# A fused decoder layer on one core: the recurrent block's input tiles ahead of its gate tiles, its products on VectorE, and a recut last norm

## The chip, the cores and the metric

The kernel runs on 1 core of a Trainium2 chip. The metric is device time in microseconds of one execution: the median of three runs for the kernel before. One more execution was recorded by the hardware profiler; all views quoted here are of that one.

## The reference

One decoder layer over 512 positions of width 1024 in float32: a norm, one wide projection, three token mixers (a chunked gMLP, a sparse attention, a gated linear recurrence), a gated sum of the three through branch weights, an output projection with a norm, and a SwiGLU block with a norm. The change touches the recurrence and the last norm above all:

```
def rglru_mixer(xr, gate, conv_w, conv_b, w_a, b_a, w_x, b_x, lam):
    xc = causal_conv4(xr, conv_w) + conv_b
    xh = xc, by heads
    r = sigmoid(einsum('bshi,hio->bsho', xh, w_a) + b_a)
    i = sigmoid(einsum('bshi,hio->bsho', xh, w_x) + b_x)
    log_a = -LRU_C * r * softplus(-lam)
    a = exp(log_a)
    b_in = sqrt(-expm1(2.0 * log_a)) * (i * xc)
    h = scan of h[t] = a[t] * h[t-1] + b_in[t]
    return h * gelu(gate)

...
f = (silu(f_gate) * f_up) @ w_ffn_out
return x + f * rsqrt(mean(f * f) + EPS) * g_post_ffn
```

(Shortened; casts are left out.)

## The kernel before

**Tiles.** Every matrix product keeps float32 accuracy by splitting both factors into a high and a low part (hi and lo, xh and xl) and adding three products: hi with xh, hi with xl, lo with xh. A tile of the projection is 128 output channels by 512 positions; with 8 blocks of the inner dimension that is 24 matmuls of 128x512 into one bank `mm` of PSUM (`passes`, L212; `matrix`, L216). The input of the projection is hh and hl, the normed x.

**Weights.** They stream tile by tile in the order of `wlist` (L124 to L161). `wload` (L166) issues the DMA of a 512 KB tile into one of two raw buffers from SyncE (SP), ScalarE (ACT) copies out hi (L114) and VectorE (DVE) subtracts lo (L119). `unit` (L201) asks for two tiles ahead.

**Order.** A list of main generators (each one a tile) and one side generator are woven by `run` (L1157): after every group of 6 matmuls the side generator may advance, at the given rate, and a tile that yields a number w is set aside and resumed w steps later, between the matmuls of the next tiles. The calls of `run` stand at L1202 to L1209. Tile's scheduler then fixes the order of instructions for each engine; each engine works through its own list in order and waits on semaphores.

**The recurrence** has 8 channel tiles in two halves of four. For each there is an input tile, `xr_tile` (L410): 24 matmuls, then a causal convolution (ACT L420, three DVE passes L422), a split into ch and cl, six matmuls L430 with the block-diagonal gate weights wabh and wabl into two `tr` banks, a sigmoid into R (L432), a tanh into TI (L435) and a DVE product with xc (L436). And there is a gate tile of the recurrence, `rg_tile` (L460): 24 matmuls and a gelu in four passes (`gelu2`, L383 to L390) into GG. Per half, `rec_batch` (L439) makes T and the decay a on ACT (tanh, sqrt, exp), a DVE product (L454), a GpSimd (POOL) product (L455) and the scan on DVE (L457); `rec_out` (L466) multiplies with GG on POOL (L473) and splits the result into ych and ycl, the input of the branch product. Input and gate tiles alternate within a half, with `gate_tile` (the three branch gates of the attention heads, L586) and two `cmp_tile` (L606, inputs of the compressed keys and values) between the halves, beside which the first half's recurrence runs.

**Around it.** `norm` (L326) finishes hh and hl under the first tiles `v_half`; `softplus` (L359) is a polynomial of some 26 small DVE operations; `compress` (L627) loads the compression weights w1 with two DMAs from ACT (L630), adds the position codes on POOL (L638) and multiplies on PE (L648 to L676); `gmlp_prep` (L480) loads two tables gw for the gMLP (L483, L484), masks one on POOL (L485) and scales the other on DVE (L487).

**The end.** `down` (L1103) accumulates the last product for four blocks of 128 rows, in two halves f of 512 columns each. `close` (L1125) squares and sums a block's rows on ACT (L1128), and in the second half forms the reciprocal root, multiplies by the gain gf and by the root, adds the residual and stores the rows.

## Time and profile before

| what | us |
|---|---|
| median of three runs | 1164.91 |
| the three runs | 1162.02, 1165.14, 1164.91 |
| the profiled execution | 1168.17 |
| its span, first to last instruction | 1166.4 |
| busy: PE, DVE, ACT, POOL | 1140.9, 690.6, 532.8, 55.2 |
| mean granted PE clock | 0.991 of full speed |

The profile's page draws the span in 40 equal slices of 29.2 us; a digit is the busy share in tenths, and PEclk the granted clock in tenths:

```profile
PE   9999799999999999999999999999999999999997
DVE  5974855545476799998898743557333323322324
POOL 0000702510000000000000000000000000000001
PEclk9999989899999999999999999999999999999999
```

PE is full but for one slice early on, the fifth (117 to 146 us), which is also the one in which POOL works most; the sixth and the eighth show a clock below the others. A timeline row reads: start, duration (both us), engine, line, operation, output <- inputs by name, shape, count, and in brackets how long the engine had been idle and what it had waited for. A row that ends in x3 sums three.

### The profile page before, as it was taken

Reading aid. Unit: us, or ns where it says so; the run is one execution under the profiler, and the core shown is the slowest. Engines: PE = TensorE matmul, PEld = TensorE weight load, DVE = VectorE, ACT = ScalarE, POOL = GpSimd, SP = SyncE. Lnnn points to the kernel's source line nnn. Section 1 sums busy time; section 2 is a strip of 40 time slices with the busy share of each in tenths; the row PEclk is TensorE's granted clock in tenths of the full one; section 3 lists DMA queues with packets and bytes.
Section 4 is the critical chain, followed back from the end, with each engine's and each line's share of the span. In section 5 each row is a group of like instructions: output and inputs, shape, how many; then the busy total and the mean of one; then the engine's idle time right before and its main releaser. Section 6 shows DMA issues by size and latency. Waiting matters only on the chain.

```text
span 1166.4 us, 14306 instructions
## 1 busy us (share of the span) xinstructions
PE 1140.9 (98%) x5524; PEld 949.6 (81%) x5524; DVE 690.6 (59%) x1266; ACT 532.8 (46%) x936; POOL 55.2 (5%) x55
## 2 busy tenths in 40 slices
PE   9999799999999999999999999999999999999997
PEld 7877578788888887888888788889988888888885
DVE  5974855545476799998898743557333323322324
ACT  6746446222244576877776523344323223232222
POOL 0000702510000000000000000000000000000001
PEclk9999989899999999999999999999999999999999
DMA  8332222522222211112111343332132232232231
GB/s 286 116 108 73 69 76 65 209 92 90 94 87 91 72 55 37 55 41 69 37 55 55 110 145 107 116 119 73 55 103 96 91 106 93 92 125 91 93 106 72
DMA packets 30373, 108.62 MB, mean 93 GB/s; under 512 B 3649, under 2 KB 3793, under 8 KB 29153
## 3 DMA queue, kind: packets, MB, share of 16 engines
q1 hardware_dynamic: 27792, 98.58, 25.7%
q10 hardware_dynamic: 2448, 9.05, 2.1%
q8 instruction: 43, 0.70, 0.2%
q14 instruction: 26, 0.20, 0.1%
q0 software_dynamic: 64, 0.08, 0.0%
HBM read 105.60 MB, written 2.10 MB: 92 GB/s over the span
## 4 chain that ended last, share of the span: by engine, by line
PE 87%; DVE 7%; DMA 3%; ACT 2%; issue 1%; POOL 1%; SPq 0%; DVEq 0%; ACTq 0%; POOLq 0%
PE mm L212 57%; PE mm L1122 10%; PE mm L1022 4%; PE sc L816 3%; PE o L854 3%; PE tr L841 3%; PE mm L732 2%; DVE lo L119 1%; PE tr L648 1%; PE tr L430 1%; DMA wabr<-in_wab 1%; DMA xrow<-in_x 1%; DVE ti L457 1%; PE tr L564 1%; DMA xt<-in_xT 1%
## 5 line engine op out<-in xcount | busy, mean ns | idle before, releaser
L114 ACT ACTIVATE hi<-raw 128x1024 fp32r<-128x1024 f32 (+1 forms) x162 | 170.8, 1054 | 357.6 <-PE mm L212 160.7
L119 DVE TENSOR_TENSOR lo<-raw,hi 128x1024 fp32r<-128x1024 f32 (+1 forms) x162 | 199.6, 1233 | 220.4 <-ACT hi L114 212.6
L212 PE MATMUL mm<-hh,lo 128*128 128x512 f32 x504 | 199.5, 396 | 2.5 <-DVE lo L119 2.5
L212 PE MATMUL mm<-hh,hi 128*128 128x512 f32 x504 | 200.5, 398 | 0.0
L212 PE MATMUL mm<-hl,hi 128*128 128x512 f32 x504 | 198.8, 395 | 0.0
L212 PE MATMUL mm<-fh,hi 128*128 128x512 f32 (+1 forms) x336 | 127.6, 380 | 0.0
L212 PE MATMUL mm<-fh,lo 128*128 128x512 f32 (+1 forms) x336 | 127.3, 379 | 0.0
L212 PE MATMUL mm<-fl,hi 128*128 128x512 f32 (+1 forms) x336 | 127.3, 379 | 0.0
L212 PEld LDWEIGHTS mm<-hh,lo 128*128 128x128 f32 x504 | 95.7, 190 | 22.8 <-DVE lo L119 3.4
L212 PEld LDWEIGHTS mm<-hl,hi 128*128 128x128 f32 x504 | 95.5, 189 | 18.9 <-issue 0.2
L212 PEld LDWEIGHTS mm<-hh,hi 128*128 128x128 f32 x504 | 95.6, 190 | 18.8 <-issue 0.2
L1122 PE MATMUL mm<-hi,f 128*128 128x512 f32 x320 | 99.4, 389 | 0.0
L822 ACT ACTIVATE P<-P,ast 128x128 f32<-128x128 f32 (+3 forms) x128 | 70.7, 555 | 23.2 <-DVE ast L820 22.6
L212 PEld LDWEIGHTS mm<-fh,lo 128*128 128x128 f32 x336 | 63.2, 188 | 12.0
L212 PEld LDWEIGHTS mm<-fh,hi 128*128 128x128 f32 x336 | 63.2, 188 | 11.8
L212 PEld LDWEIGHTS mm<-fl,hi 128*128 128x128 f32 x336 | 63.2, 188 | 11.7
L1122 PEld LDWEIGHTS mm<-hi,f 128*128 128x128 f32 x320 | 60.1, 188 | 12.4
L820 DVE CUSTOM_DVE_ANT_0 P<-sc,mask 128x128 f32<-128x128 f32 (+3 forms) x128 | 58.0, 485 | 8.2 <-PE sc L816 7.3
L1122 PE MATMUL mm<-lo,f 128*128 128x512 f32 x160 | 62.2, 389 | 0.0
L114 ACT ACTIVATE ph<-tr 128x512 fp32r<-128x512 f32 x80 | 47.0, 592 | 26.2 <-PE tr L841 25.2
L1079 DVE TENSOR_TENSOR silu<-silu,mm 128x512 f32<-128x512 f32 x22 | 15.1, 688 | 73.1 <-PE mm L212 73.1
L119 DVE TENSOR_TENSOR pl<-tr,ph 128x512 fp32r<-128x512 f32 x80 | 54.4, 686 | 2.8 <-ACT ph L114 1.0
(295 smaller groups left out, 1941.8 us busy)
## 6 DMA issues: line engine op xcount, KB each, us to landing
raw<-in_w_in SPq DMA_DIRECT2D x64, 512.0 KB, 3.5
raw<-in_w_fi SPq DMA_DIRECT2D x44, 512.0 KB, 3.5
raw<-in_w_br SPq DMA_DIRECT2D x24, 512.0 KB, 3.5
raw<-in_w_fo SPq DMA_DIRECT2D x22, 512.0 KB, 3.5
w<-in_cw ACTq DMA_DIRECT2D x4, 1024.0 KB, 6.6
raw<-in_w_o SPq DMA_DIRECT2D x8, 512.0 KB, 3.6
...
xt<-in_xT SPq DMA_DIRECT2D x8, 256.0 KB, 7.4
```

The lines of the kernel that those rows point to most:

```text
L114: SC.activation(hi, src, AF.Copy)
L119: res["lo"] = V.tensor_sub(lo, src, f32(hi))
L212: res["mm"] = PE.matmul(ps[:m, n0:n1], w[:, k * 128:k * 128 + m], x[k][:, n0:n1], start=(t == 0), stop=(t == 3 * NK - 1))
L732: PE.matmul(ps, x[k][:, q], w[:, ws], start=(k == 0 and t == 0), stop=(k == NK - 1 and t == 2))
L816: PE.matmul(ps[:, :w * n].rearrange("p (b n) -> p b n", b=w), lhs, K[:, i, brs[0]:brs[-1] + 1, :n], start=(i == 0), stop=(i == 1))
L820: V.tensor_tensor_reduce(out=t, in0=ps[:, b * n:b * n + n], in1=mask[0][:, S - n:], scale=-0.125, scalar=3.0e38, op0=OP.add, op1=OP.min, a ...
L822: SC.activation(t, t, AF.Exp, scale=-1.0, bias=st[:, 0, j, b:b + 1], accum_out=st[:, 1, j, b:b + 1])
L841: PE.transpose(pt[:, j * 128:(j + 1) * 128], self.part(j, br)[:, kt * 128:(kt + 1) * 128], ident)
L854: PE.matmul(po, VV[:, kt, g % 2, br].rearrange("p i d -> p (i d)"), x, start=(br == 0 and kt == 0 and t == 0), stop=(br == 1 and kt == a a ...
L1022: res["mm"] = PE.matmul(b[c, f], x[k][:, q], w[:, fs], start=(k == 0 and t == 0), stop=(k == NK - 1 and t == 2))
L1079: V.tensor_mul(s, s, pu)
L1122: PE.matmul(b[c], x[k][:, q], w[:, ws], start=(k == 0 and t == 0), stop=(k == NFF - 1 and t == 2))
```

## The change

Eight things change:

- The recurrence's tiles go in another order, in `run` and in `wlist` alike: the four input tiles of the first half and the attention's gate tile; then the four rg tiles of the first half, one cmp tile and the four input tiles of the second half, with the first half's recurrence beside them; then the four rg tiles of the second half, two cmp tiles and the first compression, with the second half's recurrence beside them. A tile's gate products are asked for one step later (`yield 4`).
- The two products of the recurrence on POOL (L455, L473) go to DVE.
- `softplus` runs inside `norm`, beside the first tiles, no longer beside the first half's tiles.
- The result pair yc is kept in a slab per half, and R of the second half takes another slab.
- At the start, the vec table is loaded from SP and the first half of the first weight tile from ACT; the second weight tile is asked for earlier; 11 in place of 9 warm-up products.
- The small tables of both compressions are loaded at once from POOL's queue.
- The gw tables of the gMLP are loaded from POOL's queue, no longer from SP's.
- In the last norm, gf is scaled by -0.5 beforehand, both halves are multiplied by gf on DVE straight from PSUM, the square root is taken of the second half's sum with the first half's as bias, one shorter Newton step follows (its factor of -2 meets the -0.5), and the last store is cut in three.

The diff, without the pieces on `rsqrt` (its form for the last norm goes), on the warm-up count and on the old place of `wload(1)`:

```diff
--- before.py
+++ after.py
@@ -132,9 +132,10 @@
             wlist.append((A["w_br"][i, j], None))
 
     wlist += [(A["w_v"][i], None) for i in range(8)]
-    w_in(T_CMP, *range(8))
+    w_in(T_CMP, *range(T_XR, T_XR + 8, 2))
     wlist.append((A["w_gate"], "gate"))
-    w_in(T_CMP + 1, T_CMP + 2, *range(8, 16), T_CMP + 3)
+    w_in(*range(T_XR + 1, T_XR + 8, 2), T_CMP + 1, *range(T_XR + 8, T_XR + 16, 2), *range(T_XR + 9, T_XR + 16, 2),
+         T_CMP + 2, T_CMP + 3)
 
     w_in(T_MG + 16, T_MG + 17)
     for j in range(8):
...
@@ -170,7 +171,7 @@
             raw = stage.tile([128, 1024], F32, tag="raw", name=nm("raw"), bufs=2)
             parts = [slice(0, 512), slice(512, 1024)] if i == 0 else [slice(0, 1024)]
             for n, p in enumerate(parts):
-                SY.dma_start(raw[:, p], ap[:, p])
+                (SC if i == n == 0 else SY).dma_start(raw[:, p], ap[:, p])
                 if i == 0:
                     x_in(n + 1)
             if tag == "gate":
...
@@ -233,7 +234,8 @@
 
     x_in(0)
     vec = const0([128, NVEC], "vec")
-    SC.dma_start(vec, A["vec"])
+    SY.dma_start(vec, A["vec"])
+    wload(1)
     ones = const0([128, 128], "ones")
     V.memset(ones, 1.0)
     warm = const.tile([128, 1], F32, name="warm")
...
@@ -334,7 +327,9 @@
             V.tensor_scalar(rmul[:, 1, q], rstd[:, q], GELU_C, None, op0=OP.mult)
             V.tensor_mul(rmul[:, 2, q], rstd[:, q], rstd[:, q])
             yield
+        few = softplus()
         for _ in range(19):
+            next(few, None)
             yield
         rb = bank("tr")
         with tc.issue_after(res["mm"].ins):
...
@@ -409,7 +404,7 @@
 
     def xr_tile(b, c):
         if c == 0:
-            rec[b] = dict(R=slab("r", tag="m"), GG=slab("gg", tag="m"), TI=slab("ti"))
+            rec[b] = dict(R=slab("r", tag="y" if b else "m"), GG=slab("gg", tag="m"), TI=slab("ti"))
         k = 4 * b + c
         ps = bank("mm")
         yield from matrix(ps, hh, hl)
...
@@ -423,7 +418,7 @@
         yield
         ch, cl = row("ch", F32R), row("cl", F32R)
         split(xc, ch, cl)
-        yield 3
+        yield 4
         for g, dst in ((0, "R"), (1, "TI")):
             pg = bank("tr")
             for t, (w, x) in enumerate((("hi", ch), ("hi", cl), ("lo", ch))):
...
@@ -452,7 +447,7 @@
             k = 4 * b + c
             a, t, ti = (r[n][:, c, :] for n in ("R", "T", "TI"))
             V.scalar_tensor_tensor(t, a, 1.0, t, op0=OP.add, op1=OP.mult)
-            GP.tensor_mul(t, t, ti)
+            V.tensor_mul(t, t, ti)
             yield
             V.tensor_tensor_scan(ti, a, t, 0.0, op0=OP.mult, op1=OP.add)
             yield
...
@@ -464,14 +459,14 @@
         rec[b]["gelu"] = c + 1
 
     def rec_out(b):
-        if b == 0:
-            yc["h"], yc["l"] = Pair("ych", F32R, "y"), Pair("ycl", F32R, "y")
+
+        yc["h", b], yc["l", b] = slab("ych", F32R, "y"), slab("ycl", F32R, "y")
         for c in range(4):
             while rec[b].get("gelu", 0) <= c:
                 yield
             y = row("yc32")
-            GP.tensor_mul(y, rec[b]["TI"][:, c, :], rec[b]["GG"][:, c, :])
-            split(y, yc["h"][4 * b + c], yc["l"][4 * b + c])
+            V.tensor_mul(y, rec[b]["TI"][:, c, :], rec[b]["GG"][:, c, :])
+            split(y, yc["h", b][:, c, :], yc["l", b][:, c, :])
             yield
 
 
...
@@ -480,8 +475,8 @@
     def gmlp_prep():
         gw = slab("gw", tag="wab", shape=(3, S)).rearrange("p i (g t) -> p i g t", g=G)
         wsT, rwb = gm["ws"], gm["rwb"] = gw[:, 0], gw[:, 1:3]
-        SY.dma_start(wsT, A["wsT"])
-        SY.dma_start(rwb[:, 1], A["bs"])
+        GP.dma_start(wsT, A["wsT"])
+        GP.dma_start(rwb[:, 1], A["bs"])
         GP.affine_select(wsT, wsT, pattern=[[0, G], [1, 128]], compare_op=OP.is_ge, fill=0.0,
                          base=0, channel_multiplier=-1)
         V.tensor_scalar(rwb[:, 1], rwb[:, 1], 0.5, None, op0=OP.mult)
...
@@ -628,10 +623,10 @@
         w1 = [slab("w1", tag="wab", shape=(8, 256)) for _ in range(2)]
         for i in range(2):
             SC.dma_start(w1[i], A["cw1"][kv, :, 8 * i:8 * i + 8, :])
-        w2 = mid.tile([128, 2, 64], F32, tag="cw2", name=nm("cw2"), bufs=1)
-        (GP if kv == 0 else SC).dma_start(w2, A["cw2"][kv])
-        pe = mid.tile([128, 1, 32], F32, tag="cpe", name=nm("cpe"), bufs=1)
-        (GP if kv == 0 else SC).dma_start(pe[:, 0], A["cpe"][kv])
+        w2 = const0([128, 2, 64], nm("cw2"))
+        GP.dma_start(w2, A["cw2"][kv])
+        pe = const0([128, 1, 32], nm("cpe"))
+        GP.dma_start(pe[:, 0], A["cpe"][kv])
         X = [slab("x1", shape=(G, 8, 32)), comp[kv]]
         for i in range(2):
             for g in range(G):
...
@@ -1108,6 +1103,8 @@
             for i in range(2):
                 SC.dma_start(res["gf"][i], bass.AP(tensor=A["grow"].tensor, offset=A["grow"].offset + 2 * D + 512 * i,
                                                    ap=[[0, 128], [1, 512]]))
+
+                V.tensor_scalar(res["gf"][i], res["gf"][i], -0.5, None, op0=OP.mult)
             res["y"] = Pair("yo", tag="y")
             with tc.issue_after(res["silu"].ins):
                 SC.activation(warm, warm, AF.Sqrt)
...
@@ -1123,23 +1120,30 @@
                               stop=(k == NFF - 1 and t == 2))
 
         def close(c):
+
+            ss = res["ss"]
             y = res["y"].t[f][:, c, :]
             j = row("junk")
-            SC.activation(j, b[c], AF.Square, accum_out=res["ss"][:, f, c:c + 1])
+            SC.activation(j, b[c], AF.Square, accum_out=ss[:, f, c:c + 1])
+            V.tensor_mul(y, b[c], res["gf"][f])
             if f == 0:
-                V.tensor_mul(y, b[c], res["gf"][f])
-            else:
-                ss = res["ss"]
-                V.tensor_add(ss[:, 0, c:c + 1], ss[:, 0, c:c + 1], ss[:, 1, c:c + 1])
-                i = rsqrt(ss[:, 2, c:c + 1], ss[:, 0, c:c + 1], 1, 1.0 / D, EPS, root=True)
-                with tc.issue_after(i.ins):
-                    SC.activation(y, b[c], AF.Copy)
-                GP.tensor_mul(y, y, res["gf"][f])
-                for i in range(2):
-                    y = res["y"].t[i][:, c, :]
-                    fs = slice(i * 512, i * 512 + 512)
-                    V.scalar_tensor_tensor(y, y, ss[:, 2, c:c + 1], res["x"][c][:, fs], op0=OP.mult, op1=OP.add)
-                    (SY if i else SC).dma_start(out[c * 128:(c + 1) * 128, fs], y)
+                V.tensor_scalar(ss[:, 3, c:c + 1], ss[:, 0, c:c + 1], 1.0 / D, EPS, op0=OP.mult, op1=OP.add)
+                return
+            t = const.tile([128, 3], F32, tag="cl", name=nm("cl"), bufs=2)
+            root, a, u = (t[:, i:i + 1] for i in range(3))
+            r = ss[:, 2, c:c + 1]
+            SC.activation(root, ss[:, 1, c:c + 1], AF.Sqrt, scale=1.0 / D, bias=ss[:, 3, c:c + 1])
+            V.tensor_scalar(a, ss[:, 1, c:c + 1], 1.0 / D, ss[:, 3, c:c + 1], op0=OP.mult, op1=OP.add)
+            V.reciprocal(r, root)
+
+            V.scalar_tensor_tensor(u, r, a, r, op0=OP.mult, op1=OP.mult)
+            V.scalar_tensor_tensor(r, u, -3.0, r, op0=OP.add, op1=OP.mult)
+            cut = [(1, 0, 512), (0, 0, 512)] if c < 3 else [(1, 0, 512), (0, 0, 256), (0, 256, 512)]
+            for n, (i, lo, hi) in enumerate(cut):
+                y = res["y"].t[i][:, c, lo:hi]
+                fs = slice(i * 512 + lo, i * 512 + hi)
+                V.scalar_tensor_tensor(y, y, r, res["x"][c][:, fs], op0=OP.mult, op1=OP.add)
+                (SC if n == 1 else SY).dma_start(out[c * 128:(c + 1) * 128, fs], y)
 
         for i in range(n - last):
             hi, lo = unit()
...
@@ -1187,8 +1191,8 @@
             for _ in g:
                 yield 1
 
-    def rnn(b, c0, c1):
-        return [t(b, c) for c in range(c0, c1) for t in (xr_tile, rg_tile)]
+    def four(tile, b):
+        return [tile(b, c) for c in range(4)]
 
     def qkv(g):
         return [q_tile(g, 0), q_tile(g, 1), k_tile(g)] + ([v_pair(g // 2)] if g % 2 == 0 else [])
...
@@ -1200,10 +1204,11 @@
         return r
 
     run([v_half(0), v_half(1), cmp_tile(0)], seq(norm(), load_wab()))
-    run(rnn(0, 0, 4), softplus())
-    run([gate_tile(), cmp_tile(1), cmp_tile(2)], seq(rec_batch(0), rec_out(0)))
-    run(rnn(1, 0, 4))
-    run([cmp_tile(3), gate_part("c", 0), compress(0), gate_part("c", 1)], seq(rec_batch(1), rec_out(1)))
+    run(four(xr_tile, 0) + [gate_tile()])
+    run(four(rg_tile, 0) + [cmp_tile(1)] + four(xr_tile, 1), seq(rec_batch(0), rec_out(0)), 0.45)
+    run(four(rg_tile, 1) + [cmp_tile(2), cmp_tile(3), gate_part("c", 0), compress(0), gate_part("c", 1)],
+        seq(rec_batch(1), rec_out(1)), 0.45)
+    yc["h"], yc["l"] = ([yc[n, k // 4][:, k % 4, :] for k in range(NK)] for n in "hl")
     ahead = [x for j in range(8) for x in [branch_part("c", j, yc)] + ([gate_part("c", j + 2)] if j < 6 else [])]
     run(ahead, seq(compress(1), gmlp_prep(), v_norm()))
     run([u_tile(j) for j in range(8)])
```

How the instructions of an engine stand in order, at the places that the prediction speaks of. The number behind a name counts the buffers in the order in which the program asks for them; lines of the changed kernel are five lower than before in this part of the code (L430 is L425, L422 is L417, L483 is L478).

On PE, the first gate products of the second half. Before: mm_1164 is the first rg tile of the second half, mm_1205 its second input tile, ch_1160 the convolved input of its first input tile.

```order
L212 MATMUL mm_1164<-hl_122,hi_1069 128x512
L430 MATMUL tr_1189<-ch_1160,wabh_495 128x512
L212 MATMUL mm_1164<-hh_120,lo_1070 128x512
L212 MATMUL mm_1205<-hh_119,hi_1127 128x512
L430 MATMUL tr_1189<-cl_1161,wabh_495 128x512
L430 MATMUL tr_1189<-ch_1160,wabl_496 128x512
```

After: mm_1119 is the second input tile of the second half, mm_1178 the third, ch_1115 the convolved input of the first.

```order
L213 MATMUL mm_1119<-hh_127,lo_1031 128x512
L213 MATMUL mm_1178<-hh_126,hi_1071 128x512
L213 MATMUL mm_1178<-hl_128,hi_1071 128x512
L213 MATMUL mm_1178<-hh_126,lo_1072 128x512
L213 MATMUL mm_1178<-hh_126,hi_1071 128x512
L213 MATMUL mm_1178<-hl_128,hi_1071 128x512
L213 MATMUL mm_1178<-hh_126,lo_1072 128x512
L213 MATMUL mm_1178<-hh_126,hi_1071 128x512
L425 MATMUL tr_1163<-ch_1115,wabh_523 128x512
L425 MATMUL tr_1172<-ch_1115,wabh_523 128x512
L213 MATMUL mm_1178<-hl_128,hi_1071 128x512
```

So these products stood at the end of the one tile that follows their input tile, an rg tile; now they stand seven matmuls into the second tile behind it, and all three are input tiles.

On DVE, the second half's first input tile, xc_1155 before and xc_1106 after. Before, from a weight tile's lo on:

```order
L119 TENSOR_TENSOR lo_1168<-raw_1165,hi_1167 128x1024
L422 SCALAR_TENSOR_TENSOR xc_1155<-mm_1124,vec,xc_1155 128x511
L422 SCALAR_TENSOR_TENSOR xc_1155<-mm_1124,vec,xc_1155 128x510
L422 SCALAR_TENSOR_TENSOR xc_1155<-mm_1124,vec,xc_1155 128x509
L119 TENSOR_TENSOR cl_1161<-xc_1155,ch_1160 128x512
```

After, with rows of the first half's result (yc, ycl) around it:

```order
L119 TENSOR_TENSOR ycl_1089<-yc_164_1090,ych_1088 128x512
L468 TENSOR_TENSOR yc_166_1111<-ti_627,gg_626 128x512
L119 TENSOR_TENSOR lo_1123<-raw_1120,hi_1122 128x1024
L417 SCALAR_TENSOR_TENSOR xc_1106<-mm_1068,vec,xc_1106 128x511
L119 TENSOR_TENSOR ycl_1089<-yc_166_1111,ych_1088 128x512
L417 SCALAR_TENSOR_TENSOR xc_1106<-mm_1068,vec,xc_1106 128x510
L417 SCALAR_TENSOR_TENSOR xc_1106<-mm_1068,vec,xc_1106 128x509
L119 TENSOR_TENSOR lo_1182<-raw_1179,hi_1181 128x1024
L119 TENSOR_TENSOR cl_1116<-xc_1106,ch_1115 128x512
```

Before, the three passes of the convolution followed one another, and the split cl came right behind; now two splits ycl, a product yc (which was POOL's) and the lo of a weight tile stand among them.

On DVE again, the end of the norm: hl_121 before and hl_128 after are the low part of the normed x. Before:

```order
L346 SCALAR_TENSOR_TENSOR h_57_392<-xt_79,vec,rbs_180 128x512
L346 SCALAR_TENSOR_TENSOR h_58_402<-xt_79,vec,rbs_180 128x512
L390 SCALAR_TENSOR_TENSOR vt_191<-gs_342,mm_194 128x512
L390 SCALAR_TENSOR_TENSOR vt_191<-gs_359,mm_195 128x512
L119 TENSOR_TENSOR hl_121<-h_57_392,hh_119 128x512
L119 TENSOR_TENSOR hl_121<-h_58_402,hh_119 128x512
L346 SCALAR_TENSOR_TENSOR h_59_412<-xt_79,vec,rbs_180 128x512
L119 TENSOR_TENSOR lo_419<-raw_416,hi_418 128x1024
```

After:

```order
L385 SCALAR_TENSOR_TENSOR vt_191<-gs_387,mm_195 128x512
L341 SCALAR_TENSOR_TENSOR h_57_420<-xt_79,vec,rbs_180 128x512
L341 SCALAR_TENSOR_TENSOR h_58_430<-xt_79,vec,rbs_180 128x512
L341 SCALAR_TENSOR_TENSOR h_59_440<-xt_79,vec,rbs_180 128x512
L119 TENSOR_TENSOR hl_128<-h_57_420,hh_126 128x512
L119 TENSOR_TENSOR hl_128<-h_58_430,hh_126 128x512
L119 TENSOR_TENSOR hl_128<-h_59_440,hh_126 128x512
L119 TENSOR_TENSOR lo_447<-raw_444,hi_446 128x1024
```

The three h and the three hl now stand as a block ahead of the weight tile's lo, which followed a single h before.

More of the change, by code (lines that the diff above doesn't have):

```diff
@@ L256, in hybrid_block, with rsqrt @@
                      channel_multiplier=1)
-    epsb = const.tile([128, 1], F32, name="epsb")
-    V.memset(epsb, EPS)
-    def rsqrt(dst, src, n, scale, eps, root=False):
+    def rsqrt(dst, src, n, scale, eps):
         a = const.tile([128, 8], F32, tag="rs_a", name=nm("rs_a"), bufs=2)[:, :n]
@@ L266, in rsqrt @@
         V.tensor_scalar(a, src, scale, eps, op0=OP.mult, op1=OP.add)
-        if root:
-            first = SC.activation(t, src, AF.Sqrt, scale=scale, bias=epsb)
-            V.reciprocal(dst, t)
-        else:
-            V.tensor_scalar(ib, a.bitcast(I32), 1, None, op0=OP.logical_shift_right)
-            V.tensor_scalar(dst.bitcast(I32), ib, -1.0, float(0x5F3759DF), op0=OP.mult, op1=OP.add)
-        for _ in range(1 if root else 3):
+        V.tensor_scalar(ib, a.bitcast(I32), 1, None, op0=OP.logical_shift_right)
+        V.tensor_scalar(dst.bitcast(I32), ib, -1.0, float(0x5F3759DF), op0=OP.mult, op1=OP.add)
+        for _ in range(3):
             V.tensor_mul(t, dst, dst)
@@ L276, in rsqrt @@
             V.scalar_tensor_tensor(dst, t, 1.5, dst, op0=OP.add, op1=OP.mult)
-        return first if root else None
     def spread(ps, col):
@@ L286, in hybrid_block @@
     pw = bank("mm")
-    for _ in range(9):
+    for _ in range(11):
         PE.matmul(pw[:, :128], ones, ones, start=True, stop=True)
@@ L298, in scaled @@
         V.scalar_tensor_tensor(gl[k], xt[k], g, f32(gh[k]), op0=OP.mult, op1=OP.subtract)
-    wload(1)
     x_in(3)
@@ L1125, in close @@
         def close(c):
+            ss = res["ss"]
             y = res["y"].t[f][:, c, :]
             j = row("junk")
-            SC.activation(j, b[c], AF.Square, accum_out=res["ss"][:, f, c:c + 1])
+            SC.activation(j, b[c], AF.Square, accum_out=ss[:, f, c:c + 1])
+            V.tensor_mul(y, b[c], res["gf"][f])
             if f == 0:
-                V.tensor_mul(y, b[c], res["gf"][f])
-            else:
-                ss = res["ss"]
-                V.tensor_add(ss[:, 0, c:c + 1], ss[:, 0, c:c + 1], ss[:, 1, c:c + 1])
-                i = rsqrt(ss[:, 2, c:c + 1], ss[:, 0, c:c + 1], 1, 1.0 / D, EPS, root=True)
-                with tc.issue_after(i.ins):
-                    SC.activation(y, b[c], AF.Copy)
-                GP.tensor_mul(y, y, res["gf"][f])
-                for i in range(2):
-                    y = res["y"].t[i][:, c, :]
-                    fs = slice(i * 512, i * 512 + 512)
-                    V.scalar_tensor_tensor(y, y, ss[:, 2, c:c + 1], res["x"][c][:, fs], op0=OP.mult, op1=OP.add)
-                    (SY if i else SC).dma_start(out[c * 128:(c + 1) * 128, fs], y)
+                V.tensor_scalar(ss[:, 3, c:c + 1], ss[:, 0, c:c + 1], 1.0 / D, EPS, op0=OP.mult, op1=OP.add)
[14 more added lines that the diff above has]
+                (SC if n == 1 else SY).dma_start(out[c * 128:(c + 1) * 128, fs], y)
         for i in range(n - last):
```

## The prediction

> **What bounds the kernel now.** I read the page first, for the busy shares, then the list of waits of the matmul engine (columns: total us, times, longest us), then the chain of work that ended last.
>
> ```profile
> PE 1140.9 (98%) x5524; PEld 949.6 (81%) x5524; DVE 690.6 (59%) x1266; ACT 532.8 (46%) x936; POOL 55.2 (5%) x55
> PE tr L430 <- ACT ch L114: 6.5, 2, 5.5
> PE tr L648 <- DMA w<-in_cw: 2.9, 1, 2.9
> PE mm L212 <- DVE lo L119: 2.5, 2, 1.9
> PE tr L601 <- ACT gsig L597: 0.8, 1, 0.8
> 663.02 87.08 PE mm L212 x384
> ```
>
> PE is busy 98% of the span, so only what makes PE wait, or run slowly, has a price. The chain gives the pace of a fed PE: 87.08 us for 384 matmuls, 0.227 us each, 5.45 us for a tile of 24. The four waits all lie in the recurrence stretch, but their 12.7 us are not the whole loss. For that I laid windows over the stretch and compared each window's length with what its matmuls need at that pace (columns: length, then busy us and count of PE, weight loads, DVE, ACT, POOL, then the granted PE clock, DMA share, GB/s).
>
> ```profile
> 40.00:60.00 20.00, 20.00 (x90) 16.57 (x89) 19.99 (x30) 12.91 (x19) 0.00 (x0) 1.00 0.29 98
> 60.00:70.00 10.00, 8.94 (x40) 7.10 (x39) 9.39 (x28) 2.72 (x4) 0.00 (x0) 1.00 0.36 120
> 120.00:130.00 10.00, 8.55 (x39) 6.42 (x38) 9.97 (x9) 4.69 (x7) 7.61 (x5) 1.00 0.16 52
> 130.00:140.00 10.00, 8.12 (x29) 6.25 (x28) 8.65 (x11) 3.79 (x7) 8.58 (x9) 0.83 0.17 52
> 140.00:152.00 12.00, 6.54 (x18) 4.92 (x17) 7.78 (x9) 4.65 (x7) 3.56 (x3) 0.72 0.43 132
> 200.00:214.00 14.00, 11.14 (x47) 9.47 (x46) 11.47 (x11) 3.43 (x6) 10.86 (x7) 0.76 0.50 187
> 213.66 1.61 PE L648 MATMUL tr<-xcmp,w 128*128 128x124 f32 x13
> ```
>
> Losses: 60 to 70, 10 - 40 x 0.227 = **0.9**. 120 to 130, four of the 39 are short transposes at about 0.12, so 10 - 7.9 - 0.5 = **1.6**. 130 to 140, 10 - 6.6 = **3.4**. 140 to 152, 12 - 4.1 = **7.9**. 200 to 214, 27 long ones and 20 of L648 at 1.61 / 13 = 0.124: 14 - 6.1 - 2.5 = **5.4**. Together **19.2 us**. The window from 40 to 60 loses nothing, though DVE is full there. The reasons stand in the timeline (start, duration, engine; in brackets the idle time before and what ended it).
>
> ```profile
> 126.34 2.31 DVE L457 TENSOR_TENSOR_SCAN ti<-r,t 128x512 f32<-128x512 f32 x1
> 131.68 1.23 DVE L457 TENSOR_TENSOR_SCAN ti<-r,t 128x512 f32<-128x512 f32 x1 [1.19 <-POOL t L455]
> 134.08 0.50 PE L212 MATMUL mm<-hh,lo 128*128 128x512 f32 x1 [1.88 <-DVE lo L119]
> 135.24 4.04 POOL L638 TENSOR_TENSOR x<-xcmp,cpe 128x256 f32<-128x256 f32 x4
> 136.35 0.63 PE L212 MATMUL mm<-hh,lo 128*128 128x512 f32 x1
> 136.78 0.63 PE L212 MATMUL mm<-hh,hi 128*128 128x512 f32 x1
> 145.53 0.63 ACT L114 ACTIVATE ch<-xc 128x512 fp32r<-128x512 f32 x1 [3.72 <-DVE xc L422]
> 146.21 0.80 PE L430 MATMUL tr<-ch,wabh 128*128 128x512 f32 x1 [5.46 <-ACT ch L114]
> 201.72 0.82 ACTq L630 DMA_DIRECT2D w<-in_cw  x2
> w<-in_cw ACTq DMA_DIRECT2D x4, 1024.0 KB, 6.6
> ```
>
> The same scan takes 2.31 us beside POOL's products and 1.23 us without; DVE also stands waiting for POOL's t. So DVE falls behind, lo comes 1.88 us late, PE then steps at 136.78 - 136.35 = 0.43 us, half speed (clock 0.83 in that window), and ch of the second half's first tile comes 5.46 us late. At 201.72 the compress weights are only issued when they are needed; they take 6.6 us to land.
>
> [...]
>
> **The change, part by part.** Lines are those of before. *What goes.* (1) The products of L455 and L473 go from POOL to DVE, at about the 0.68 us of L436 below. DVE gains 16 x 0.68 = 11 us over some 140 us and loses the doubled scan and the hand-overs. (2) All four input tiles of a half now precede their rg tiles, so the recurrence has its inputs early, and gate products stand a tile or more behind their own input tile. (3) Three tiles and more (over 16 us) stand between the issue of the compress weights and their use, against a landing of 6.6 us. The causes of all 19.2 us are removed: **-19.2**. It can give back less; that is in the new waits.
>
> *New waits.* The rows for an input tile's path:
>
> ```profile
> L114 ACT ACTIVATE hi<-raw 128x1024 fp32r<-128x1024 f32 (+1 forms) x162 | 170.8, 1054 | 357.6 <-PE mm L212 160.7
> L119 DVE TENSOR_TENSOR lo<-raw,hi 128x1024 fp32r<-128x1024 f32 (+1 forms) x162 | 199.6, 1233 | 220.4 <-ACT hi L114 212.6
> 77.89 0.76 ACT L420 ACTIVATE xc<-mm,vec 128x512 f32<-128x512 f32 x1
> 79.16 2.31 DVE L422 SCALAR_TENSOR_TENSOR xc<-mm,vec,xc 128x511 f32<-128x511 f32 x3
> 73.49 0.68 ACT L435 ACTIVATE ti<-tr,half 128x512 f32<-128x512 f32 x1
> 74.23 0.68 DVE L436 SCALAR_TENSOR_TENSOR ti<-ti,xc 128x512 f32<-128x512 f32 x1
> 63.81 0.17 DVE L372 TENSOR_TENSOR lt<-lt 128x8 f32<-128x8 f32 x1
> ```
>
> a) The softplus polynomial moves under the first tiles: 26 DVE operations at 0.17 = 4.4 us. And one lo of v_half now stands behind a block of three h and three hl operations, 6 x 0.68 = 4.1 us, where a single h came between hl and lo before. It is needed a tile (5.45) after its hi: 1.05 (hi) + 4.1 + 1.23 = 6.4, 0.9 late if the buffers give no lead. Taken **0.6**, bounds 0 to 1.4.
>
> b) Input tiles in a row. From the end of a tile's matmuls to ch: 0.76 + 2.31 + 0.63 = 3.7 us, and its gate products stand one tile (5.45) behind. But ACT and DVE also pass the work of neighbouring tiles to one another in a fixed order: hi 1.05, xc 0.76, two sigmoid-like passes 0.68 each, L436 0.68, two L422 1.5, ch 0.63, about 6.0, with hand-overs 6.6 to 6.8, against PE's 5.45 + 6 x 0.227 = 6.8 per tile. It just fits. Taken **0.3**, bounds 0 and 1.5 (0.4 at each of four).
>
> c) The gate tile's sigmoid: its wait of 0.8 stays in kind, now behind the last input tile's passes. **0.5**, 0 to 0.9.
>
> d) The second half's input tiles meet the first half's recurrence on DVE. DVE there holds 4 gate tiles x (2 x 0.68 + 1.23) + 1.9 for cmp + 4 input tiles x (2.31 + 2 x 0.68 + 1.23) + 4 x (4 x 0.68 + 1.23) of recurrence = 10.4 + 1.9 + 19.6 + 15.8 = **47.7 us**, against PE's 5 x 5.45 + 4 x 6.8 = **54.5**. It is 88% full, and compress's POOL adds (two groups of 4.04 as above) fall among it, since the slab they fill is free only then. The path in order: xc, one L422, one ycl, two L422, ch: 0.76 + 2.99 + 0.63 = 4.4; cl, behind a lo, 5.7; the gate products stand a tile and 7 matmuls behind, 7.0. So a backlog of 1.3 us is covered. What was 5.46 becomes **1.5**; bounds 0 and 5.5.
>
> e) A late lo in rg03 and rg13, where recurrence passes stand ahead of it: **0.6**, 0 to 1.5 (below the 1.88 seen). f) Half speed after such a wait: the window 130 to 140 lost 3.4, of which 1.9 is the wait, so 1.5 to 3.4 if it comes; **0.6**.
>
> g) The gMLP weights (gw) are loaded from POOL's queue and no longer SP's.
>
> ```profile
> gw<-in_wsT SPq DMA_DIRECT2D x1, 256.0 KB, 2.7
> cw<-in_cw POOLq DMA_DIRECT2D x1, 64.0 KB, 4.8
> cw<-in_cw ACTq DMA_DIRECT2D x1, 64.0 KB, 1.9
> ```
>
> No POOL load of that size is in the trace; the small one took 4.8 from POOL against 1.9 from ACT, 2.9 more. Behind it wait the affine select and, on DVE, L487 and the copies that PE's L676 needs, 24 matmuls (5.45 us) after the slot comes free; 2.7 + 2.9 = 5.6 and two passes more. **0.5**, 0 to 3.5. SP's weight stream gains by it; I count that nothing, since SP's next raw load is two tiles early.
>
> [...]
>
> New waits together: 0.6 + 0.3 + 0.5 + 1.5 + 0.6 + 0.6 + 0.5 = **+4.6**; all at their upper ends about 18.
>
> *The start.* The vec load goes to SP and half of the first raw tile to ACT's queue; the two more warm-up products lie in PE's wait for the first tile; the compression's small tables go to POOL's queue, where nothing else is under way then. Nothing.
>
> *The tail.*
>
> ```profile
> 1159.20 0.19 ACT L1128 ACTIVATION_READ_ACCUMULATOR junk<-mm 128x1 f32 x1
> 1159.63 0.29 ACT L268 ACTIVATE rs_t<-ss,epsb 128x1 f32<-128x1 f32 x1 [0.23 <-DVE ss L1133]
> 1159.95 0.16 DVE L269 RECIPROCAL ss<-rs_t 128x1 f32<-128x1 f32 x1 [0.17 <-ACT rs_t L268]
> 1160.54 1.22 DVE L276 SCALAR_TENSOR_TENSOR ss<-rs_t,ss 128x1 f32<-128x1 f32 x1
> 1161.80 1.42 DVE L1141 SCALAR_TENSOR_TENSOR yo<-yo,ss,xr 128x512 f32<-128x512 f32 x2
> ```
>
> The sqrt follows the accumulator directly, 1159.41 and not 1159.63, the reciprocal then ends about 1159.9; two one-column operations without POOL beside them end about 1160.35, so the first output product starts 1160.4 and not 1161.80, 1.4 earlier. The last transfer is half as wide. **-1.5**, bounds 0 and -2.0. The added scaling of gf on DVE, at most 3.3 us there, hides under lo tiles made two units (10.9 us) ahead.
>
> **The sum** against the profiled run's own 1168.17 us (span 1166.4, 1.8 around it): 1168.17 - 19.2 - 1.5 + 4.6 = 1152.1. That run is 0.28% above the median of 1164.91, so on the median's scale 1152.1 x 1164.91 / 1168.17 = **1149**.
>
> **Rivals.** *Everything is covered*: no new wait, 1168.17 - 20.7 = 1147.5, on the scale 1144.3; and 2 us less if the small stalls outside the stretch shrink too. For it: 40 to 60 shows DVE full with no loss. Against: the seven places are tight ones. *The wait returns at the second half's input tiles*: d at 5.5, half speed behind it 3.4 in place of 0.6, the others as taken: 4.0 + 2.8 = 6.8 more, 1156; with e and b at their ends 1158. For it: 88% of DVE and POOL's adds, beside which two-input passes take 1.9 times as long. Against: POOL has 8 us there, not the 19.8 of the windows from 120 to 152. *POOL's load comes late*, g at 3.5: 1152. *The change doesn't do what it says*: the losses only move, and 10 to 20 us of waits come elsewhere: 1159 to 1168. *DVE becomes the bound (slower)*: from the first gate tile to the last input tile of the second half DVE would need more than PE. Being slower than before by over 0.3% takes 54.5 + 19.5 = 74 us, 1.55 times its 47.7; at the scan's 1.9 times for all of it, 91 us, it would be 1149 + 36 = 1185. For it: the row of 126.34. Against: its cause, POOL's products, is gone, and the adds of 8 us could stretch it by 8 x 0.9 / 1.9 = 4 us.
>
> **How the numbers follow.** A measurement of this kernel tells about 0.3% from no change, 3.5 us: bounds 1161.4 and 1168.4. Forecast (1146 to 1153) 0.52; covered (1142 to 1146) 0.14; second-half wait (1153 to 1159) 0.18; POOL's load 0.05; does not do what it says 0.06, most of it above 1159; slower 0.05. The range 1142 to 1158 leaves out the last two, and 0.03 of the others. Faster 0.90, same 0.05, slower 0.05.
>
> **What would show it.** Right: the granted clock 1.00 through the stretch of the recurrence, no wait of PE for ch or for w of L648 above 1 us, scans at 1.23, the L276 of 1.22 gone from the tail. Step d wrong: PE waiting for ch or cl in the second half with DVE full before it. Step g wrong: L676 waiting behind gw. Part b wrong: equal waits of each input tile, of either half. Wrong as a whole: a lost PE time of over 12 us in the new stretch.

## The result, and the profile after

| kernel | runs | median us | range us |
|---|---|---|---|
| before | 4 | 1163.98 | 1162.02 to 1165.14 |
| after | 4 | 1145.21 | 1145.06 to 1145.44 |

The ratio is 0.9841, with a 95% interval of 0.9824 to 0.9858: 1.6% faster, 18.8 us. The profiled execution took 1145.06 us, of which its span is 1143.3 (before: 1168.17 and 1166.4).

The page after, its row of busy times, and the waits of PE inside the recurrence that are left (columns: total us, times, longest us):

```profile
PE 1132.6 (99%) x5528; PEld 945.4 (83%) x5528; DVE 687.1 (60%) x1284; ACT 530.9 (46%) x932; POOL 24.0 (2%) x39
PE tr L425 <- DVE cl L119: 0.3, 1, 0.3
PE mm L213 <- DVE lo L119: 0.2, 1, 0.2
```

The 6.5 us for ch, the 2.9 for the compression's weights and the 2.5 for lo are gone. The windows at the places of before, and for the last one the place to which the compression's products have moved (columns: length, then busy us and count of PE, weight loads, DVE, ACT, POOL, then PE clock, DMA share, GB/s):

```profile
60.00:70.00 10.00, 10.00 (x44) 7.77 (x43) 6.49 (x8) 4.76 (x6) 0.00 (x0) 1.00 0.31 105
120.00:130.00 10.00, 9.93 (x45) 7.90 (x43) 9.74 (x14) 5.50 (x7) 0.00 (x0) 1.00 0.33 105
130.00:140.00 10.00, 9.71 (x43) 7.63 (x42) 9.89 (x13) 7.51 (x11) 7.47 (x8) 1.00 0.33 105
140.00:152.00 12.00, 12.00 (x53) 9.53 (x52) 7.60 (x11) 8.51 (x14) 0.00 (x0) 1.00 0.16 45
180.00:200.00 20.00, 20.00 (x123) 17.45 (x122) 11.22 (x14) 8.00 (x14) 5.94 (x6) 1.00 0.52 189
```

The counts tell it: 43 matmuls where there were 29, 53 where there were 18, and the clock is 1.00 in each. DVE is still full from 120 to 140 (9.74 and 9.89 us of 10.00), but PE's longest wait for it there is 0.3 us. The last window holds the compression's products, now fed (20.00 of 20.00 us busy).

For the size of a change within the stretch I use two fixed points of the program: the first matmul of the first cmp tile, and the first product with gw, behind which both programs run alike. Before and after (start, duration):

```profile
52.37 0.39 PE L212 MATMUL mm<-gxh,hi 128*128 128x512 f32 x1
...
256.47 1.02 PE L491 MATMUL tr<-gw,ones 128*128 128x512 f32 x2
```

```profile
51.28 0.39 PE L213 MATMUL mm<-gxh,hi 128*128 128x512 f32 x1
...
234.71 1.02 PE L486 MATMUL tr<-gw,ones 128*128 128x512 f32 x2
```

The stretch went from 204.10 to 183.43 us, 20.7 less. Ahead of it 1.1 went, behind the last matmul 1.1 (7.72 to 6.61), and 0.2 in between: 23.1, the difference of the two profiled executions. The same two points in every run below:

| kernel | what is different | median us | stretch us |
|---|---|---|---|
| before | | 1163.98 | 204.10 |
| before, second profile | | | 199.92 |
| after | | 1145.21 | 183.43 |
| after, again | | 1146.35 | 183.41 |
| e1 | both products on POOL | 1156.52 | 193.72 |
| e9 | only the scan's product on POOL | 1155.92 | 193.59 |
| e10 | only the outer product on POOL | 1150.98 | 188.88 |
| e2 | old order of tiles | 1155.19 | 188.46 |
| e3 | old order, both products on POOL | 1161.55 | 199.41 |
| e4 | old start | 1145.89 | 183.42 |
| e5 | old last norm | 1147.16 | 183.73 |
| e6 | softplus at its old place | 1146.59 | 184.43 |
| e7 | gw from SP's queue | 1146.66 | 183.45 |
| e8 | gate products one step earlier | 1146.28 | 183.65 |

Medians moved by about 1 us between the two sets of runs of the changed kernel; its stretch repeats to 0.02 us. So differences under 1 us are read from the stretch. Where PE waits for long it repeats less well (204.10 and 199.92 before), and each of e1 to e3, e9 and e10 has one profile.

### The profile page after: what moved, and what is told of

Read it like the earlier page. It is cut to its first block, busy times and chain, and to the rows that moved or that the text cites. A ratio compares the mean times of both kernels' runs of the same rounds, so it can differ in the third digit from the quotient of the medians.

```text
span 1143.3 us, 14308 instructions
## 1 busy us (share of the span) xinstructions
PE 1132.6 (99%) x5528; PEld 945.4 (83%) x5528; DVE 687.1 (60%) x1284; ACT 530.9 (46%) x932; POOL 24.0 (2%) x39
## 4 chain that ended last, share of the span: by engine, by line
PE 95%; DVE 3%; ACT 1%; DMA 1%; issue 0%; SPq 0%; DVEq 0%; ACTq 0%
PE mm L213 61%; PE mm L1119 10%; PE mm L1017 4%; PE mm L499 3%; PE sc L811 3%; PE o L849 3%; PE tr L836 3%; PE mm L727 2%; PE tr L643 1%; PE tr L425 1%; DMA raw<-in_w_v 1%; PE tr L559 1%; PE tr L749 1%; DVE lo L119 1%; DVE pl L119 0%; PE mm L586 0%
## 5 line engine op out<-in xcount | busy, mean ns | idle before, releaser
L213 PEld LDWEIGHTS mm<-hh,hi 128*128 128x128 f32 x504 | 94.7, 188 | 18.8 <-ACT hi L114 0.4
L817 ACT ACTIVATE P<-P,ast 128x128 f32<-128x128 f32 (+3 forms) x128 | 70.6, 554 | 23.1 <-DVE ast L815 22.5
```

The costliest lines, as they stand in the source:

```text
L213: res["mm"] = PE.matmul(ps[:m, n0:n1], w[:, k * 128:k * 128 + m], x[k][:, n0:n1], start=(t == 0), stop=(t == 3 * NK - 1))
L817: SC.activation(t, t, AF.Exp, scale=-1.0, bias=st[:, 0, j, b:b + 1], accum_out=st[:, 1, j, b:b + 1])
```

## The experiments

**The two main parts, undone one at a time and together.** e1 puts both products back on POOL:

```diff
-            V.tensor_mul(t, t, ti)
+            GP.tensor_mul(t, t, ti)
...
-            V.tensor_mul(y, rec[b]["TI"][:, c, :], rec[b]["GG"][:, c, :])
+            GP.tensor_mul(y, rec[b]["TI"][:, c, :], rec[b]["GG"][:, c, :])
```

> The changed kernel with the recurrence's two products back on POOL, its order of tiles kept. Theory P (the products on POOL, which slow DVE's passes beside them, were the main cause): a good part of the lost PE time comes back, 6 to 10 us over the 1145.2 of the changed kernel, so 1151 to 1155, with scans of 2.3 us and PE waiting for lo or ch. Rival O (the order of the tiles was the cause, the products only a symptom): within 2 us, 1145 to 1147.

e2 puts the old order of tiles back, with the products on DVE (the old weight list too):

```diff
-    run(four(xr_tile, 0) + [gate_tile()])
-    run(four(rg_tile, 0) + [cmp_tile(1)] + four(xr_tile, 1), seq(rec_batch(0), rec_out(0)), 0.45)
-    run(four(rg_tile, 1) + [cmp_tile(2), cmp_tile(3), gate_part("c", 0), compress(0), gate_part("c", 1)],
-        seq(rec_batch(1), rec_out(1)), 0.45)
+    run(rnn(0, 0, 4))
+    run([gate_tile(), cmp_tile(1), cmp_tile(2)], seq(rec_batch(0), rec_out(0)))
+    run(rnn(1, 0, 4))
+    run([cmp_tile(3), gate_part("c", 0), compress(0), gate_part("c", 1)], seq(rec_batch(1), rec_out(1)))
```

> The changed kernel with the order of tiles of before (input and gate tiles alternating, the old four calls and weight list, yield 3), the products on DVE. Theory P: the wait for ch of the second half (5.5) and the lo waits are gone, only the wait for the compression's weights with its half speed (5.4) stays: about 1150 to 1151. Rival O: nearly the whole loss comes back, 1158 to 1162.

e3 does both:

> Both undone: the old order and the products on POOL, with the new start, tail, softplus place and table loads. What remains of the gain is start (1.1) and tail (1.1): about 1162 beside the 1164.0 of before. If softplus or the table loads carry part of the gain, it is lower, 1155 to 1160.

Measured beside before: e1 1156.52 (ratio 0.9932, 0.9918 to 0.9947), e2 1155.19 (0.9926, 0.9909 to 0.9942), e3 1161.55 (0.9981, 0.9971 to 0.9990). In the stretch e1 costs 10.3 us, e2 5.0, e3 16.0. Neither theory is right alone: the products are worth two thirds, the order one third, and in the stretch they nearly add (15.3 against 16.0). e1 is 1.5 us above theory P's range, with the waits that P named: 6.8 us for lo, 0.8 for ch. In e2 the median lies between the two theories. P's 5 to 6 us fit its stretch, but not by P's mechanism: P had the waits for lo and ch gone and the compression's left, and e2 waits 1.3 us for lo, 1.7 for ch, 1.3 for ycl, and not for the compression. The rest of e2's 10 us in its median is not in the stretch. Far behind it a tile stands waiting for a bank of PSUM:

```profile
342.57 0.79 PE L212 MATMUL mm<-hh,hi 128*128 128x512 f32 x1 [3.26 <-DVE u L384]
```

That wait, and half speed behind it (granted clock 0.91 in the window 330 to 345, 0.98 from 345 to 360, and 1.00 at the same place after), make some 5 us, by estimate. No other kernel here has it; e3 and before have the same order of tiles without it, so it isn't the order alone; what brings it stays open.

e2 also answers where the compression's wait came from. Its two loads are issued, ACT's queue in e2:

```profile
182.52 0.34 ACTq L624 DMA_DIRECT2D w<-in_cw  x1
...
187.60 0.33 ACTq L624 DMA_DIRECT2D w<-in_cw  x1
```

and PE waits for neither (the first of these products starts at 191.48). In e3, with POOL's products back, ACT issues both at once, behind a copy that had waited 2.85 us for DVE, and PE waits again (timeline, then list of waits):

```profile
199.17 0.65 ACT L617 ACTIVATE xcmp<-mm 64x256 f32<-64x256 f32 x1 [2.85 <-DVE xcmp L618]
199.18 0.82 ACTq L624 DMA_DIRECT2D w<-in_cw  x2
```

```profile
PE tr L642 <- DMA w<-in_cw: 2.5, 1, 2.5
```

So the late DMA comes with DVE's backlog, seen through ACT. But the backlog isn't all of it. In e2 the scheduler has also put the first load ahead of that copy, where e3 has it behind. Issued with the second at 187.60, and landing in the 5.08 us of e3 (199.18 to 204.26), it would have come 1.2 us late, by estimate. And the new order is enough without the products: in e1, with both on POOL, the two loads are issued at 166.37 and 182.02, the first product starts at 193.73, and PE doesn't wait.

**Which of the two products.** e9 puts only the one that the scan reads on POOL, e10 only the outer one (each is one line of e1's diff).

> The changed kernel with only the recurrence's inner product (the one whose result the scan reads) back on POOL. Theory H (hand-over: DVE, which works in order, stands waiting for POOL's product with a weight tile's lo queued behind the scan): nearly all of the 10 us of both products, 1154 to 1156, with PE waiting for lo. Rival C (contention alone: each product slows the passes beside it, eight of each kind): about half, 1150 to 1152.

> The changed kernel with only the recurrence's outer product (with the gelu branch, read by a split on ACT and DVE) back on POOL. Theory H: next to nothing, within 1.5 us of the changed kernel, 1145 to 1147.5. Rival C: about half of the 10 us, 1150 to 1152.

e9: 1155.92 (0.9934, 0.9919 to 0.9949), as theory H had it. e10: 1150.98 (0.9893, 0.9879 to 0.9908), as the rival had it; H gave it 1.5 at most, and was wrong there. The inner product alone brings the whole 10.2 us, the outer one alone 5.5, both together no more than the inner one. In e9, POOL's row of the first two products, and DVE's rows of the first half's recurrence:

```profile
101.96 2.93 POOL L450 TENSOR_TENSOR t<-t,ti 128x512 f32<-128x512 f32 x2 [97.59 <-DVE t L449]
```

```profile
101.18 1.30 DVE L449 SCALAR_TENSOR_TENSOR t<-r,t 128x512 f32<-128x512 f32 x2 [4.56 <-ACT r L444]
103.67 2.30 DVE L452 TENSOR_TENSOR_SCAN ti<-r,t 128x512 f32<-128x512 f32 x1 [1.19 <-POOL t L450]
105.90 0.66 DVE L449 SCALAR_TENSOR_TENSOR t<-r,t 128x512 f32<-128x512 f32 x1
106.49 0.67 DVE L383 SCALAR_TENSOR_TENSOR gs<-gs,mm 128x512 f32<-128x512 f32 x1
107.08 1.91 DVE L452 TENSOR_TENSOR_SCAN ti<-r,t 128x512 f32<-128x512 f32 x1
108.92 1.19 DVE L119 TENSOR_TENSOR lo<-raw,hi 128x1024 fp32r<-128x1024 f32 x1
```

and the same place after:

```profile
99.91 1.31 DVE L449 SCALAR_TENSOR_TENSOR t<-r,t 128x512 f32<-128x512 f32 x2 [4.56 <-ACT r L444]
101.13 1.29 DVE L450 TENSOR_TENSOR t<-t,ti 128x512 f32<-128x512 f32 x2
102.34 0.68 DVE L383 SCALAR_TENSOR_TENSOR gs<-gs,mm 128x512 f32<-128x512 f32 x1
102.93 1.22 DVE L452 TENSOR_TENSOR_SCAN ti<-r,t 128x512 f32<-128x512 f32 x1
104.07 1.20 DVE L119 TENSOR_TENSOR lo<-raw,hi 128x1024 fp32r<-128x1024 f32 x1
```

From the start of the first row to the start of lo it is 7.74 us in e9 and 4.16 after. Three things make the 3.6: DVE stands 1.19 us for POOL; the scan beside POOL takes 2.30 in place of 1.22 (the next 1.91); and the scheduler has put one more row of L449 (0.66) and the second scan ahead of lo. In return the two products, 1.29 together, are gone from DVE. PE pays twice, once in each half (e9, first half; brackets: idle time and what ended it):

```profile
110.17 0.50 PE L213 MATMUL mm<-hh,lo 128*128 128x512 f32 x1 [3.11 <-DVE lo L119]
...
110.74 0.54 PE L213 MATMUL mm<-hl,hi 128*128 128x512 f32 x1
111.08 0.63 PE L213 MATMUL mm<-hh,lo 128*128 128x512 f32 x1
```

The waits for lo sum to 6.8 us, and half speed behind each (granted clock 0.91 in the window 100 to 120, 0.94 from 152 to 180) makes up most of the rest, by estimate.

In e10 no scan waits for POOL; passes of DVE beside it are slowed (a lo to 2.32 us, where the next one took 1.21), and the input tile's ch is late (POOL, DVE, ACT, then PE):

```profile
110.74 1.60 POOL L468 TENSOR_TENSOR yc<-ti,gg 128x512 f32<-128x512 f32 x1 [3.56 <-ACT hi L114]
111.10 2.32 DVE L119 TENSOR_TENSOR lo<-raw,hi 128x1024 fp32r<-128x1024 f32 x1
...
125.33 1.43 DVE L119 TENSOR_TENSOR lo<-raw,hi 128x1024 fp32r<-128x1024 f32 x1
...
129.91 0.63 ACT L114 ACTIVATE ch<-xc 128x512 fp32r<-128x512 f32 x1 [4.27 <-DVE xc L417]
```

```profile
130.59 1.22 PE L425 MATMUL tr<-ch,wabh 128*128 128x512 f32 x2 [3.42 <-ACT ch L114]
```

Beside the second lo, at 125.33, POOL is in the compression's adds and not in a product; they begin at 123.62 in e10 and at 131.21 after.

Part of that wait is order, not contention: the scheduler put these gate products one matmul into the third input tile in e10 (and in e1), and seven in after and in e9, six matmuls or 1.4 us earlier. After, the same ch starts at 128.06:

```profile
128.06 0.63 ACT L114 ACTIVATE ch<-xc 128x512 fp32r<-128x512 f32 x1
```

Counted from the first cmp tile (51.14 in e10, 51.28 after) that is 76.8 us after and 78.8 in e10, 2.0 later. With the 1.4 these make up the wait of 3.4. So the rival had the number of e10, and contention alone explains some 2.0 of the 3.4; no run separates the two.

What POOL's products cost DVE's passes beside them, by the rows: a lo took 2.32 us (e10) in place of 1.20 to 1.23 (after), the scan 2.30 (e9) in place of 1.22 (after).

**The small parts.** The changed kernel was run again beside them, without an edit.

> The changed kernel itself, unaltered, as the reference for small differences on this chip: 1145.2 again, within 0.5.

e4, the old start:

```diff
-                (SC if i == n == 0 else SY).dma_start(raw[:, p], ap[:, p])
+                SY.dma_start(raw[:, p], ap[:, p])
...
-    SY.dma_start(vec, A["vec"])
-    wload(1)
+    SC.dma_start(vec, A["vec"])
...
-    for _ in range(11):
+    for _ in range(9):
...
+    wload(1)
     x_in(3)
```

> The changed kernel with the old start (vec from ACT's queue, the whole first weight tile from SP's, the second tile asked for later, 9 warm-up products). My prediction gave the start nothing; the traces have the first cmp tile begin 1.09 us earlier after the change. Theory: 1.1 slower, 1146.3. Rival (the earlier begin comes from elsewhere, or is lost again behind it): 1145.2.

e5, the last norm: `close` and `rsqrt` as they stood before, and gf not scaled ahead.

```diff
-                V.tensor_scalar(res["gf"][i], res["gf"][i], -0.5, None, op0=OP.mult)
...
-            V.tensor_mul(y, b[c], res["gf"][f])
...
+                with tc.issue_after(i.ins):
+                    SC.activation(y, b[c], AF.Copy)
+                GP.tensor_mul(y, y, res["gf"][f])
```

> The changed kernel with the old last norm (root form, product on POOL, two stores a block). My prediction gave the new tail 1.5 us; the traces have 7.73 us from the last matmul's end to the span's end before and 6.61 after. Theory: 1.1 slower, 1146.3; by my sum 1146.7. Rival (the end is set by the last transfer, not by the row operations): 1145.2.

e6, softplus beside the first input tiles again:

```diff
-        few = softplus()
         for _ in range(19):
-            next(few, None)
...
-    run(four(xr_tile, 0) + [gate_tile()])
+    run(four(xr_tile, 0) + [gate_tile()], softplus())
```

> The changed kernel with the softplus polynomial beside the first half's input tiles again, where it stood before. Theory: before the change it caused the wait of 1.2 us for ch at 68 us, so with the input tiles in a row it costs about that again: 1146.4. Rival (DVE has room there, as the products behind an input tile stand a whole tile later now): 1145.2; if my term a (0.6 lost under the first tiles) was real, 1144.6.

e7, gw from SP:

```diff
-        GP.dma_start(wsT, A["wsT"])
-        GP.dma_start(rwb[:, 1], A["bs"])
+        SY.dma_start(wsT, A["wsT"])
+        SY.dma_start(rwb[:, 1], A["bs"])
```

> The changed kernel with the two gw loads issued from SP's queue as before. If POOL's queue made them late and PE waited: 0.5 (my term g) to 2.5 faster, 1142.7 to 1144.7. If they are hidden either way: 1145.2. If the SP queue's weight tiles are held up by them: slower, up to 1146.

e8, the gate products one step earlier:

```diff
-        yield 4
+        yield 3
```

> The changed kernel with an input tile's gate products asked for one step earlier (yield 3, as before). My term b held that the input tiles in a row just fit (6.6 to 6.8 us of ACT and DVE against PE's 6.8 per tile). If so, the earlier products make PE wait for ch at each of eight input tiles, 0.5 to 1 us each: 1149 to 1153. Rival (the path to ch, 3.7 us, has room within one tile of 5.45): 1145 to 1147.

Measured: after again 1146.35 (1145.32 to 1146.74; ratio to before beside it 0.9849), 1.1 over the first time, where 0.5 was expected. e4 1145.89, from 1144.78 to 1147.55; e5 1147.16; e6 1146.59; e7 1146.66; e8 1146.28.

- *e4, the start.* The first cmp tile starts at 51.27 with the old start, at 51.28 and 51.59 with the new, and at 52.53 in e7, whose start is the new one too. So the 1.1 us between the two first profiles can't be put down to the new start; what moves it by a microsecond from run to run stays open.
- *e5, the last norm.* From the start of the last matmul to the span's end 8.0 us (1136.90 to 1144.9) against 7.0 after (1136.30 to 1143.3); 0.8 us between medians. The rows of e5 that the change removes:

```profile
1139.15 1.22 DVE L278 SCALAR_TENSOR_TENSOR ss<-rs_t,ss 128x1 f32<-128x1 f32 x1
1140.41 1.41 DVE L1144 SCALAR_TENSOR_TENSOR yo<-yo,ss,xr 128x512 f32<-128x512 f32 x2
```

- *e6, softplus.* The stretch is 1.0 us longer: PE waits again where it did before, at the first gate products:

```profile
68.49 0.73 PE L423 MATMUL tr<-ch,wabh 128*128 128x512 f32 x2 [0.80 <-ACT ch L114]
```

  So softplus's new place gains a microsecond. The medians (0.24 apart) can't show it.
- *e7, gw.* 183.45 against 183.41 and 183.43: hidden from either queue. After, from POOL's queue, the DMA issue's row (KB, us to landing):

```profile
gw<-in_wsT POOLq DMA_DIRECT2D x1, 256.0 KB, 3.0
```

  It takes 3.0 us from POOL against 2.7 from SP before; in these 3.0 us, from 217.63 on, DVE runs only one product of 0.69 us and the start of a lo.
- *e8, gate products earlier.* 183.65, 0.2 us longer, with no wait for ch. The path to ch has room within one tile in the first half, where the products did move (by 1 to 16 matmuls). At the second half's first tile the scheduler left them seven matmuls into the third tile, as after, so there the run says nothing.

**The kernel before, profiled again.**

> The kernel before once more, for a second profile of it. Theory: the waits of PE are the same as in the first profile to some tenths, and its runs, which spread over 3 us and more where the changed kernel's spread over 0.4, differ by whether PE drops to half speed behind a wait. So a span nearer 1162, with the same waits and a mean granted clock above 0.991. Rival: the waits themselves differ.

The kernel is unchanged. It took 1164.76 us, with a span of 1163.1 and a mean clock of 0.996 (0.991 in the first profile). Its PE rows at the two large waits:

```profile
134.00 0.50 PE L212 MATMUL mm<-hh,lo 128*128 128x512 f32 x1 [1.83 <-DVE lo L119]
134.33 0.40 PE L212 MATMUL mm<-hh,hi 128*128 128x512 f32 x1
...
146.12 0.79 PE L430 MATMUL tr<-ch,wabh 128*128 128x512 f32 x1 [7.07 <-ACT ch L114]
```

Behind the wait for lo, the same as in the first profile (1.83 against 1.88), PE steps at full speed this time (0.24 and 0.23 us from 134.33 on, where it was 0.43 in the first profile). It reaches the gate products 1.7 us earlier, and waits 7.07 us for ch instead of 5.46; the wait ends at 146.12 against 146.21. So theory and rival are both half right: the half speed differs, but there it cost nothing, since DVE sets when ch comes (ACT had stood 3.80 us for DVE's xc before ch). It cost most behind the compression's wait, where no later wait hides it: the window 200 to 214 has 78 matmuls here at a clock of 1.00, 47 in the first profile at 0.76 (short ones and long).

```profile
200.00:214.00 14.00, 11.27 (x78) 10.02 (x77) 11.45 (x11) 4.25 (x7) 11.38 (x8) 1.00 0.50 188
```

The stretch is 199.92 us against 204.10. Of the 4.2 us between them 2.8 come behind the compression's wait, 0.9 between the wait for ch and that one (half speed behind ch lasts 5.3 us in the first profile, 4.0 here), and 0.5 ahead. That is most of why the first profile's execution was 4 us above the median.

## Why the prediction was right, point by point

It named 1149, a range of 1142 to 1158, and faster; measured were 1145.2, then 1146.4. Both lie between the forecast and the rival "everything is covered" (1144.3), and nearer to the rival; the first is in the rival's band (1142 to 1146), which had been given 0.14. The mechanism held: the granted clock is 1.00 in the windows, the eight scans take 1.21 to 1.22 us, and PE waits for ch and for the compression's weights no longer. The sizes were further off than the time shows: on the profiled run's own scale the sum gave 1152.1, and the profiled execution took 1145.06. Of these 7.0 us, 3.5 are in the new waits (point 3), 2.6 in the loss (1), 1.1 in the start (4), 0.2 between stretch and tail, and the tail (5) takes 0.4 off.

1. *The loss.* "The causes of all 19.2 us are removed": right. The windows' count was 19.2; the stretch became 20.7 shorter with new waits of 1.1 in it (point 3), so 21.8 went. The other 2.6 stood at the windows' edges and in small gaps outside them.
2. *Its causes.* Three were named side by side. The runs rank them: POOL's products 10.3 us, the order 5.0, and the late weights of the compression are no third beside them: the wait is gone with either of the two alone (e1, e2) and back without both (e3).
3. *The new waits*, predicted at +4.6, are the step that was mis-sized. (a) softplus and the block of h and hl, +0.6: nothing of it shows. e6, without softplus under the norm, starts the first cmp tile at 51.21, after at 51.28 and 51.59, though that start moves by 1 us from run to run. The 1.0 us that e6 loses is no gain to set against this: it is the 0.9 of the window 60 to 70, which the 19.2 hold already. (b) Input tiles in a row, "it just fits", +0.3: there is room in the first half (e8), and no wait for ch in either. (c) The gate tile's sigmoid, +0.5: no such wait is left in the list. (d) The second half's input tiles, +1.5: 0.7 of delay, one place at 128.3 and one at 137.6 (0.2 and 0.5 above the usual spacing). (e) The late lo, +0.6: 0.4, at 161.4. (f) Half speed, +0.6: none, the clock is 1.00. (g) gw, +0.5: none (e7); the 2.5 us that e7's expectation allowed at most is shown by no run, the stretch differs by 0.04 at most. Together 1.1 in place of 4.6.
4. *The start*, predicted nothing: 1.1 us less in the first pair of profiles, but e4 has it with the old start, so it isn't shown to be the change's.
5. *The tail*, -1.5: -1.1 by the traces. The 0.4 that is missing stands in DVE's rows after:

```profile
1136.30 0.39 PE L1119 MATMUL mm<-hi,f 128*128 128x512 f32 x1
...
1137.22 0.19 ACT L1127 ACTIVATION_READ_ACCUMULATOR junk<-mm 128x1 f32 x1
1137.44 0.69 DVE L1128 TENSOR_TENSOR yo<-mm,gf 128x512 f32<-128x512 f32 x1 [2.66 <-ACT junk L1127]
1137.44 0.29 ACT L1135 ACTIVATE cl<-ss 128x1 f32<-128x1 f32 x1
1138.05 0.20 DVE L1136 TENSOR_SCALAR cl<-ss 128x1 f32<-128x1 f32 x1
1138.17 0.15 DVE L1137 RECIPROCAL ss<-cl 128x1 f32<-128x1 f32 x1
...
1138.81 1.54 DVE L1145 SCALAR_TENSOR_TENSOR yo<-yo,ss,xr 128x512 f32<-128x512 f32 x3
```

   The square root did come right behind the accumulator, and is done at 1137.73. But DVE is in the product with gf until 1138.05, and the reciprocal waits behind it: I had moved that product to DVE in the sum without queueing it there.
6. *The scale.* I took the profiled run's excess over the median as a factor of 0.28%, 3.2 us. It was a lump, for the most part half speed behind the compression's wait, that the second profile (1164.76) lacks. So 19.2 was the loss of that execution and about 15 that of the second; the factor took off about as much, 3.2, for a reason that was wrong. That it brought 1152.1 to 1149, nearer to what was measured, is luck.
7. *The rivals.* DVE as the bound: DVE is at 97% and 99% in the windows 120 to 140 and PE at 99% and 97%, so these 20 us are close to it. Over the whole overlap, 93 to 148, DVE is busy 46.0 of 55.0 us, 84%, where the sum had 47.7 of 54.5, 88%. The input-tile wait with half speed came in e10 (3.42 us, clock 0.68 in the window 130 to 140), not in the changed kernel. The 1.9 times that this rival gave to passes beside POOL's adds are the scan's beside POOL's products; beside the adds a lo took 1.64 us after (at 135.53, otherwise 1.20 to 1.23) and a cl 1.10 (at 137.10, otherwise 0.69), 1.3 and 1.6 times.
